# A conv-FFN up-projection with a second convolution buffer, an earlier copy-out and a reordered weight load

## The chip, the cores and the metric

The kernel runs on one core of a Trainium2 chip. The metric is the time of one execution on the device in microseconds, the median of several; lower is better. The core has five instruction queues: PE (matrix products, with its weight loads as PEld), DVE (vector), ACT (scalar), POOL (GpSimd) and SP, which here only issues DMAs. Each queue runs its instructions in order, and an instruction that has to wait for another engine holds up all that stands behind it in its own queue.

## The reference, cut to what matters

One layer of a hybrid streaming encoder, on 1024 prompt frames and 8 x 16 sampled frames (1152 rows in all, float32):

```python
mixed = sigmoid(gate_a) * o_gla + sigmoid(gate_b) * o_diff       # two token mixers
x = layer_norm(ALPHA * x + mixed @ w_out, ln1_g, ln1_b)          # (1152, 1024)

up = x @ w_up                                                    # (1152, 2 * 2816)
a, gate = split(up, [2816])
a_full = concat([left, a], axis=time)                            # two earlier rows
a_conv = conv_b
for j in range(3):
    a_conv = a_conv + a_full[:, j:j + t] * conv_w[j]
h = gelu(a_conv) * gate
x = layer_norm(ALPHA * x + h @ w_down, ln2_g, ln2_b)
```

The change lies in the middle part: from `x` after the first layer norm to `h`.

## The kernel before

Up to about 1,220 us the kernel computes the mixers; nothing of that is touched. Then come three stages.

**Output projection.** A loop over nine tiles `t` of 128 rows: `mixed @ w_out` on PE, `layer_norm`, transposes on PE, and copies of the transposed rows into the arrays from which the up-projection's moving operands are made. From `t = 4` on, four additions and subtractions per tile (L946 to L949, on POOL) combine the row halves in place (`rs1`, `r21`, `r11`, `r12`). Between the tiles the code already puts in pieces of the first two up-projection panels: `Panel(0)` (a weight load and two casts with their splits) at `t = 6`; `panels[0].sums()` (a second load and the weight sums) and `Panel(1)` at `t = 7`; the first and second product of panel 0 at `t = 8`, and the first product of panel 1 after it.

**Up-projection.** 22 panels `f` of 128 columns of `a` and 128 of `gate`. A panel is a two-by-two block scheme with seven products in place of eight. Every product has two halves `c`, four steps of depth, and three matmuls each (high and low parts of a float32 split): 24 matmuls of 128x288, so 168 in a panel. The sums over the product numbers are kept in PSUM: tile `ux` takes up products 1, 6, 7 and 4 in turn, `uy` product 2, `uz` products 5 and then 3. What is read out on the way:

- after product 1: `first_out` copies `ux` into the convolution's input `ab` on ACT (L798), and adds `uy` (product 2) on DVE (L800). Product 6 may not write over `ux` before the copy is done. Ahead of that the two left-edge columns are set on POOL (L795, L796).
- after product 6: ACT copies `ux` into the gate tile `gt` (L806); after product 7 again (L811), and DVE adds `uz` (L812).
- after product 4: ACT copies `ux` into the second half of `ab` (L815, L817); after product 3 DVE adds `uz` to `gt` (L819).
- then the convolution on DVE, `ab` to `cv` (L825 to L829), its gelu on ACT (L830), the product with `gt` on DVE (L831), and the store of `h_d[f]` (L832).

The weights of a panel are two loads of 512 KB, issued by SP (L746 and L758, three buffers in `wpool`), four sums on POOL (L762 to L765), and for each of the seven products a cast on ACT (L93) and a split on DVE (L96). The five weights of products 6, 5, 7, 4 and 3 go through a ring of `WV` buffers (tag `wv`), those of 1 and 2 through three (`w0`). There is one `ab` (pool `ue`), one `gt` and one `cv` (pool `uc`).

**Down-projection.** `h` is read back, cast and split (`hw`), and multiplied with `w_down` in six groups of panels, the first with two.

The order of each engine's queue is not the order of the code: the framework simulates the program on a timeline and sorts the instructions by it (`schedule_with_timeline_sim=True`); waits are put in afterwards. In the steady panels PE's queue before is, with the number of matmuls behind each product (n is a panel, n+1 the next): 5 of n, 24; 6 of n, 24; 2 of n+1, 11; 7 of n, 24; 2 of n+1, 11; 4 of n, 24; 3 of n, 24; 2 of n+1, 2; 1 of n+2, 24. In the code, `rest` runs from product 6 to the store.

## Time and profile before

| what | value |
|---|---|
| time, median of 3 runs (lowest to highest) | 2195.18 us (2193.39 to 2195.99) |
| the profiled execution | 2196.83 us |
| its span | 2195.1 us |
| granted clock of PE, mean | 0.984 |
| PE busy | 2083.5 us, 95% |
| PE weight loads busy | 1953.6 us, 89% |
| DVE busy | 1165.0 us, 53% |
| ACT busy | 785.0 us, 36% |
| POOL busy | 468.3 us, 21% |

The profiled execution lies 1.65 us above the median of the runs, and its span is 1.7 us shorter than its time. PE is busy for 95% of the span, so all that can be won without fewer matmuls is in the other 112 us and in stretches with a lower clock. The up-projection takes the span from about 1,337 to 1,899 us, the down-projection the rest. In the profile's rows a number such as `128x288` is a tile (partitions x elements); `[1.73 <-ACT ab L798]` says that the engine stood idle for 1.73 us just before, and that the event that ended it was the ACT instruction of line 798 that writes `ab`. Where a row ends in `x2`, two instructions are put together, and the duration is that of both.

### The profile page before, as it was taken

What the parts mean: (1) busy time and instruction counts of PE and PEld (TensorE: products, weight loads), DVE (VectorE), ACT (ScalarE), POOL (GpSimd) and SP (SyncE); (2) the same over time, 40 slices, a digit from 0 to 9 for tenths busy, and PEclk for the clock granted to TensorE, in tenths of its full rate; (3) what the DMA queues carried; (4) which work ended last, traced back from release to release, by engine and by line L of the source; (5) the groups of instructions that cost most, each with busy time, mean ns of one, the idle gap of its engine ahead of it and who ended that gap; (6) DMA issues with size and microseconds to landing.
All of it is one profiled execution on the core that took longest, in us unless ns stands there. A gap on an engine that the chain in (4) does not pass through costs nothing.

```text
span 2195.1 us, 34411 instructions
## 1 busy us (share of the span) xinstructions
PE 2083.5 (95%) x14088; PEld 1953.6 (89%) x14088; DVE 1165.0 (53%) x1848; ACT 785.0 (36%) x1750; POOL 468.3 (21%) x531
## 2 busy tenths in 40 slices
PE   7999999999999989999999895899999999999998
PEld 7999999899999989999999785899989999878886
DVE  4344443554536455554641666666666666554447
ACT  3233333344434444443644324333333333311122
POOL 0133242100120102101223025322332232000006
PEclk9999999999999999999999997999999999999999
DMA  5215322513052233314342531221212121452222
GB/s 173 55 24 113 96 75 78 134 30 97 25 133 59 59 71 71 94 46 85 58 79 100 185 115 58 62 78 60 71 60 81 61 70 61 164 172 82 82 72 87
DMA packets 187003, 185.31 MB, mean 84 GB/s; under 512 B 9318, under 2 KB 169428, under 8 KB 186830
## 3 DMA queue, kind: packets, MB, share of 16 engines
q1 hardware_dynamic: 186846, 183.11, 29.6%
q8 instruction: 111, 1.82, 0.3%
q14 instruction: 46, 0.38, 0.1%
HBM read 131.10 MB, written 51.98 MB: 83 GB/s over the span
## 4 chain that ended last, share of the span: by engine, by line
PE 50%; DVE 11%; DMA 5%; ACT 3%; issue 2%; POOL 1%; SPq 0%; DVEq 0%; ACTq 0%; POOLq 0%
PE mm L87 5%; PE mm L88 5%; PE mm L89 5%; PE ux L87 4%; PE dn L87 3%; PE dn L89 3%; PE dn L88 3%; PE ux L89 3%; PE ux L88 3%; DVE cv L828 3%; DVE wv L96 2%; PE po L657 2%; PE opp L87 1%; PE opp L89 1%; PE opp L88 1%
## 5 line engine op out<-in xcount | busy, mean ns | idle before, releaser
L88 PE MATMUL mm<-wlo,xh 128*128 128x256 f32 x1368 | 394.2, 288 | 0.6 <-DVE wlo L96 0.6
L89 PE MATMUL mm<-whi,xl 128*128 128x256 f32 x1368 | 394.1, 288 | 0.0
L87 PE MATMUL mm<-whi,xh 128*128 128x256 f32 x1368 | 393.4, 288 | 0.0
L87 PE MATMUL ux<-xh,wv 128*128 128x288 f32 x704 | 214.2, 304 | 54.8 <-ACT ab L798 32.7
L88 PEld LDWEIGHTS mm<-wlo,xh 128*128 128x128 f32 x1368 | 263.0, 192 | 3.1 <-issue 1.0
L89 PEld LDWEIGHTS mm<-whi,xl 128*128 128x128 f32 x1368 | 263.1, 192 | 2.3 <-issue 0.8
L87 PEld LDWEIGHTS mm<-whi,xh 128*128 128x128 f32 x1368 | 262.6, 192 | 2.5 <-issue 1.0
L88 PE MATMUL ux<-xl,wv 128*128 128x288 f32 x704 | 212.1, 301 | 0.0
L89 PE MATMUL ux<-xh,wv 128*128 128x288 f32 x704 | 211.6, 301 | 0.0
L87 PE MATMUL mm<-xh,whi 128*128 128x384 f32 x576 | 195.7, 340 | 3.5 <-ACT dq L233 3.3
L89 PE MATMUL mm<-xh,wlo 128*128 128x384 f32 x576 | 196.4, 342 | 0.0
L88 PE MATMUL mm<-xl,whi 128*128 128x384 f32 x576 | 196.4, 341 | 0.0
L87 PEld LDWEIGHTS ux<-xh,wv 128*128 128x128 f32 x704 | 136.1, 193 | 59.5 <-ACT ab L798 37.0
L87 PE MATMUL dn<-hw 128*128 128x512 f32 x396 | 154.2, 396 | 7.9 <-ACT hw L93 4.2
L88 PE MATMUL dn<-hw 128*128 128x512 f32 x396 | 155.3, 395 | 0.0
L89 PE MATMUL dn<-hw 128*128 128x512 f32 x396 | 153.3, 392 | 0.0
L88 PEld LDWEIGHTS ux<-xl,wv 128*128 128x128 f32 x704 | 136.4, 194 | 0.1
L89 PEld LDWEIGHTS ux<-xh,wv 128*128 128x128 f32 x704 | 136.3, 194 | 0.0
L632 ACT ACTIVATE e<-sc,mx 128x256 f32<-128x256 f32 (+7 forms) x128 | 94.0, 740 | 90.3 <-DVE mx L628 78.5
L701 POOL TENSOR_TENSOR gm<-gm,sg 128x512 f32<-128x512 f32 (+1 forms) x40 | 50.0, 1251 | 308.9 <-ACT sg L223 139.3
L87 PEld LDWEIGHTS mm<-xh,whi 128*128 128x128 f32 x576 | 108.6, 189 | 5.8 <-ACT dq L233 3.6
L96 DVE TENSOR_TENSOR wlo<-raw,whi 128x1024 fp32r<-128x1024 f32 x62 | 92.2, 1493 | 36.2 <-ACT whi L93 35.9
(325 smaller groups left out, 4778.6 us busy)
## 6 DMA issues: line engine op xcount, KB each, us to landing
fraw<-in_w_up SPq DMA_DIRECT2D x44, 512.0 KB, 3.9
raw<-in_w_in SPq DMA_DIRECT2D x38, 512.0 KB, 6.1
raw<-in_w_in SPq DMA_DIRECT2D x52, 256.0 KB, 6.1
h_d<-cv SPq DMA_DIRECT2D x22, 576.0 KB, 5.1
hr<-h_d SPq DMA_DIRECT2D x22, 576.0 KB, 3.7
fraw<-in_w_down SPq DMA_DIRECT2D x22, 512.0 KB, 4.4
og_d<-orow SPq DMA_DIRECT2D x4, 1152.0 KB, 11.3
od_d<-od SPq DMA_DIRECT2D x8, 576.0 KB, 4.5
```

What stands on the lines that cost most here:

```text
L87: nc.tensor.matmul(ps, lhsT=lh, rhs=rh, start=start, stop=False, skip_group_check=more)
L88: nc.tensor.matmul(ps, lhsT=lh, rhs=rl, start=False, stop=False, skip_group_check=more)
L89: nc.tensor.matmul(ps, lhsT=ll, rhs=rh, start=False, stop=stop, skip_group_check=more)
L96: V.tensor_tensor(lo, src, hi.bitcast(F32), ALU.subtract)
L632: act(e[:, :nk], scs[m][:, :nk], AF.Exp, bias=mx[:, m:m + 1], accum_out=Z[:, i, m:m + 1])
L657: nc.tensor.matmul(po[:, 0, :], lhsT=wT[:, kt, :], rhs=v[:, kt, vc0:vc0 + P], start=kt == 0, stop=kt == i)
L701: G.tensor_tensor(gv, gv, e, ALU.mult)
L828: V.scalar_tensor_tensor(cv[:, :SEQ], ab[:, j:j + SEQ], cw[:, j, f:f + 1], cv[:, :SEQ], ALU.mult, ALU.add)
```

## The change

Five things are edited.

1. `ab` alternates between two pools: panels with an odd number take it from `uc`, the others from `ue`, so that there are two buffers.
2. `first_out` is split: the copies of `ux` stay in it, the two additions of `uy` are in a new `second_out`. The calls are now `first_out`, `second`, `second_out`: the first product is copied out ahead of the second product.
3. The ring `wv` of weight buffers has six tiles, not seven (`WV = 6`).
4. `Panel(0)` stands at `t = 5` and `Panel(1)` at `t = 6`; `panels[0].sums()` stays at `t = 7`.
5. At the last tile of the output projection the four combinations of rows run on DVE and not on POOL.

```diff
@@ -42,7 +42,7 @@
 WB = 256
 HT = NTOK // 2
 HN = HT // 2
-WV = 7
+WV = 6
 PREP_AT = 6
 
 
@@ -790,12 +790,15 @@
 
         def first_out(self):
             f = self.f
-            self.ab = ab = ue.tile([P, SEQ + 2 + NS * 18], F32, tag="ab", name="ab")
+            self.ab = ab = (uc if f % 2 else ue).tile([P, SEQ + 2 + NS * 18], F32, tag="ab", name="ab")
             self.abs_ = ab[:, SEQ + 2:].rearrange("p (s c) -> p s c", c=18)
             G.memset(ab[:, 0:2], 0.0)
             G.tensor_copy(self.abs_[:, :, 0:2], ccT[:, f])
             for c in range(2):
                 nc.scalar.copy(ab[:, 2 + c * HN:2 + (c + 1) * HN], self.X[c][:, :HN])
+
+        def second_out(self):
+            ab = self.ab
             for c in range(2):
                 V.tensor_tensor(ab[:, 2 + c * HN:2 + (c + 1) * HN], ab[:, 2 + c * HN:2 + (c + 1) * HN], self.Y[c][:, :HN], ALU.add)
 
@@ -918,15 +921,15 @@
                     nxt = o_prep(t + 1)
                     rn = r_load(t + 1)
             layer_norm(op, r, g1, b1)
-            if t == 6:
-                panels[0] = Panel(0)
+            if t in (5, 6):
+                panels[t - 5] = Panel(t - 5)
             if t == 7:
                 panels[0].sums()
-                panels[1] = Panel(1)
             if t == NT - 1:
                 panels[0].first()
+                panels[0].first_out()
                 panels[0].second()
-                panels[0].first_out()
+                panels[0].second_out()
             nc.sync.dma_start(x1_d[t * P:(t + 1) * P, :], r)
             for j in range(2):
                 tp = otp.tile([P, 512], F32, tag="otp", name="otp").rearrange("p (i c) -> p i c", i=4)
@@ -943,10 +946,11 @@
                     nc.scalar.copy(R[f"r2{j + 1}"][:, :, b - HT:hi - HT], tp[:, :, b - lo:])
             if hi > HT:
                 c = slice(max(lo, HT) - HT, hi - HT)
-                G.tensor_tensor(R["rs1"][:, :, c], R["r21"][:, :, c], R["r22"][:, :, c], ALU.add)
-                G.tensor_tensor(R["r21"][:, :, c], R["r11"][:, :, c], R["r21"][:, :, c], ALU.subtract)
-                G.tensor_tensor(R["r11"][:, :, c], R["rs1"][:, :, c], R["r11"][:, :, c], ALU.subtract)
-                G.tensor_tensor(R["r12"][:, :, c], R["r12"][:, :, c], R["r11"][:, :, c], ALU.subtract)
+                E = V if t == NT - 1 else G
+                E.tensor_tensor(R["rs1"][:, :, c], R["r21"][:, :, c], R["r22"][:, :, c], ALU.add)
+                E.tensor_tensor(R["r21"][:, :, c], R["r11"][:, :, c], R["r21"][:, :, c], ALU.subtract)
+                E.tensor_tensor(R["r11"][:, :, c], R["rs1"][:, :, c], R["r11"][:, :, c], ALU.subtract)
+                E.tensor_tensor(R["r12"][:, :, c], R["r12"][:, :, c], R["r11"][:, :, c], ALU.subtract)
             if t == NT - 1:
                 panels[1].first()
 
@@ -972,8 +976,9 @@
         if f > 1:
             p.first()
         if f > 0:
+            p.first_out()
             p.second()
-            p.first_out()
+            p.second_out()
         p.rest()
     us_.close()
     xv_s.close()
```

Lines behind `first_out` have numbers that are 3 higher in the changed kernel (the copy to `gt`, L806, is L809; the additions of `uy`, L800, are L803; the gelu is L833, the product with `gt` L834, the store L835), and those of the row combinations 4 higher. Since the queues are sorted by a simulated timeline, they move in more places than the diff names. From about `t = 5` of the output projection on the order differs; ahead of that, and behind the first group of the down-projection, it is the same. In the steady panels PE's queue is now: 6 of n, 24 matmuls; 5 of n, 24; 7 of n, 24; 1 of n+1, 11; 4 of n, 24; 3 of n, 24; 1 of n+1, 13; 2 of n+1, 24. Three more places follow; a name such as `ab_15777` is one allocation of a tile, and `[waits PE_49]` names the engine that an instruction waits for.

ACT and then DVE in a steady panel, before; `ux_15751` and `ux_15752` are the two halves of panel n+1, `cv_15710` is the convolution of panel n, `gt_15574` its gate, `uy_15777` a half of product 2 of n+1:

```order
L93 CAST wv_15972<-ta_15966 128x512 [waits Pool_49]
L93 CAST wv_15975<-ta_15966 128x512 [waits PE_49]
L93 CAST wv_16194<-fraw_16192 128x512 [waits DMAHW2_49,PE_49]
L93 CAST wv_16197<-fraw_16192 128x512 [waits PE_49,Activation_49]
L830 ACTIVATE cv_15710<-cv_15710 128x1152 [waits DMAHW3_49,DVE_49]
L798 COPY ab_15803<-ux_15751 128x288 [waits Pool_49]
L798 COPY ab_15803<-ux_15752 128x288
L93 CAST wv_15978<-tb_15967 128x512 [waits PE_49]
L806 COPY gt_15810<-ux_15751 128x288 [waits DVE_49,PE_49]
```

```order
L96 TENSOR_TENSOR wv_16194<-fraw_16192,wv_16194 128x512 [waits DMAHW2_49,Activation_49]
L96 TENSOR_TENSOR wv_16197<-fraw_16192,wv_16197 128x512 [waits Activation_49]
L831 TENSOR_TENSOR cv_15710<-cv_15710,gt_15574 128x1152 [waits Activation_49]
L800 TENSOR_TENSOR ab_15803<-ab_15803,uy_15777 128x288 [waits Activation_49]
L800 TENSOR_TENSOR ab_15803<-ab_15803,uy_15778 128x288 [waits Activation_49]
```

The same in the changed kernel, where `uy_15782` is the half of product 2 of n+1:

```order
L93 CAST wv_15972<-ta_15966 128x512 [waits PE_49,Activation_49,Pool_49]
L798 COPY ab_15777<-ux_15751 128x288 [waits PE_49]
L798 COPY ab_15777<-ux_15752 128x288 [waits PE_49]
L93 CAST wv_15961<-fraw_15956 128x512
L833 ACTIVATE cv_15710<-cv_15710 128x1152 [waits DMAHW2_49,DVE_49]
L93 CAST wv_16194<-fraw_16192 128x512 [waits DMAHW3_49,PE_49,Activation_49]
L809 COPY gt_15810<-ux_15751 128x288 [waits DVE_49,PE_49]
L809 COPY gt_15810<-ux_15752 128x288 [waits PE_49]
```

```order
L96 TENSOR_TENSOR wv_15961<-fraw_15956,wv_15961 128x512 [waits PE_49,Activation_49]
L803 TENSOR_TENSOR ab_15777<-ab_15777,uy_15782 128x288 [waits PE_49]
L803 TENSOR_TENSOR ab_15777<-ab_15777,uy_15783 128x288 [waits PE_49]
L834 TENSOR_TENSOR cv_15710<-cv_15710,gt_15574 128x1152 [waits Activation_49]
L96 TENSOR_TENSOR wv_16194<-fraw_16192,wv_16194 128x512 [waits DMAHW3_49,Activation_49]
```

On ACT the two copies to `ab` (L798) stood behind the gelu and waited for POOL; now they stand ahead of it and wait for PE, with one weight cast in front of them that waits for PE, ACT and POOL. On DVE the two additions of `uy` stood behind the product with `gt` (L831); now they stand ahead of it (L834) and wait for PE.

POOL and then SP in a steady panel, before; `ta` and `tb` are the weight sums of one panel, `fraw` its two loads:

```order
L762 TENSOR_TENSOR ta_15966<-fraw_15964,fraw_15956 128x512 [waits DMAHW7_49,DMAHW1_49]
L764 TENSOR_TENSOR tb_15967<-fraw_15964 128x512
L821 COPY tails_78<-ab_15331 128x2 [waits Activation_49]
L822 COPY tails_78<-ab_15331 128x16 [waits Activation_49]
L763 TENSOR_TENSOR ta_15966<-fraw_15964,ta_15966 128x512 [waits Pool_49]
L765 TENSOR_TENSOR tb_15967<-fraw_15956,ta_15966 128x512 [waits Pool_49]
L795 MEMSET ab_15567 128x2 [waits DVE_49]
L796 COPY ab_15567<-ccT_77 128x8x2
```

```order
L746 DMA fraw_15956<-in_w_up 128x8x128 [waits DMAHW4_49,DMAHW7_49,DVE_49,Pool_49]
L832 DMA h_d_62<-cv_15238 128x1152 [waits DVE_49]
L758 DMA fraw_15964<-in_w_up 128x8x128 [waits DMAHW3_49,DVE_49]
```

And in the changed kernel:

```order
L795 MEMSET ab_15777 128x2 [waits DVE_49,Pool_49]
L796 COPY ab_15777<-ccT_77 128x8x2
L762 TENSOR_TENSOR ta_15966<-fraw_15964,fraw_15956 128x512 [waits DMAHW1_49,DMAHW0_49]
L764 TENSOR_TENSOR tb_15967<-fraw_15964 128x512
L763 TENSOR_TENSOR ta_15966<-fraw_15964,ta_15966 128x512 [waits Pool_49]
L765 TENSOR_TENSOR tb_15967<-fraw_15956,ta_15966 128x512 [waits Pool_49]
L824 COPY tails_78<-ab_15541 128x2 [waits Activation_49]
L825 COPY tails_78<-ab_15541 128x16 [waits Activation_49]
```

```order
L746 DMA fraw_15956<-in_w_up 128x8x128 [waits DMAHW3_49,DVE_49]
L758 DMA fraw_15964<-in_w_up 128x8x128 [waits DMAHW1_49,DMAHW5_49,DVE_49,Pool_49]
L835 DMA h_d_62<-cv_15474 128x1152 [waits DVE_49]
```

The same `ab` columns, sums and tails are set, but the left-edge columns of a later panel now stand ahead of the sums, and the copies of the tails, which wait for ACT, behind them. On SP the first load of a panel (L746) now waits for DVE alone and the second (L758) for DVE and POOL; before it was the other way round.

POOL at the turn from the output projection into the panels, before; `rs1`, `r21`, `r11` and `r12` are the combinations of tile 6 (its last two) and of tile 7, `fraw_13465` and `fraw_13358` the loads of panel 0, `fraw_13866` and `fraw_13473` those of panel 1:

```order
L765 TENSOR_TENSOR tb_13468<-fraw_13358,ta_13467 128x512 [waits Pool_49]
L948 TENSOR_TENSOR r11_12635<-rs1_12634,r11_12635 128x4x128 [waits Pool_49]
L949 TENSOR_TENSOR r12_12631<-r12_12631,r11_12635 128x4x128 [waits Pool_49]
L762 TENSOR_TENSOR ta_13868<-fraw_13866,fraw_13473 128x512 [waits DMAHW5_49,DMAHW7_49,DVE_49,PE_49]
L764 TENSOR_TENSOR tb_13869<-fraw_13866 128x512 [waits PE_49]
L763 TENSOR_TENSOR ta_13868<-fraw_13866,ta_13868 128x512 [waits Pool_49]
L946 TENSOR_TENSOR rs1_12634<-r21_12632,r22_12633 128x4x128 [waits Activation_49]
L765 TENSOR_TENSOR tb_13869<-fraw_13473,ta_13868 128x512 [waits Pool_49]
L947 TENSOR_TENSOR r21_12632<-r11_12635,r21_12632 128x4x128 [waits Pool_49]
L948 TENSOR_TENSOR r11_12635<-rs1_12634,r11_12635 128x4x128 [waits Pool_49]
L949 TENSOR_TENSOR r12_12631<-r12_12631,r11_12635 128x4x128 [waits Pool_49]
```

And in the changed kernel, where `fraw_13473` and `fraw_13259` are the loads of panel 0, `fraw_13866` and `fraw_13366` those of panel 1:

```order
L952 TENSOR_TENSOR r11_12635<-rs1_12634,r11_12635 128x4x128 [waits Pool_49]
L762 TENSOR_TENSOR ta_13475<-fraw_13473,fraw_13259 128x512 [waits DMAHW2_49,DMAHW5_49,DVE_49,PE_49]
L764 TENSOR_TENSOR tb_13476<-fraw_13473 128x512 [waits PE_49]
L953 TENSOR_TENSOR r12_12631<-r12_12631,r11_12635 128x4x128 [waits Pool_49]
L763 TENSOR_TENSOR ta_13475<-fraw_13473,ta_13475 128x512 [waits Pool_49]
L765 TENSOR_TENSOR tb_13476<-fraw_13259,ta_13475 128x512 [waits Pool_49]
L950 TENSOR_TENSOR rs1_12634<-r21_12632,r22_12633 128x4x128 [waits Activation_49]
L762 TENSOR_TENSOR ta_13868<-fraw_13866,fraw_13366 128x512 [waits DMAHW0_49,DMAHW7_49,DVE_49,PE_49]
L764 TENSOR_TENSOR tb_13869<-fraw_13866 128x512 [waits PE_49]
L951 TENSOR_TENSOR r21_12632<-r11_12635,r21_12632 128x4x128 [waits Pool_49]
L763 TENSOR_TENSOR ta_13868<-fraw_13866,ta_13868 128x512 [waits Pool_49]
```

The sums of panel 0 (L762 to L765) have gone from between the first combinations of tile 6 to behind them, and those of panel 1 from ahead of the combinations of tile 7 to between them. The four combinations of tile 8, which stood behind all this on POOL, are no longer in its queue.

## Rows read from the trace of the kernel before

**Rows 1.** Waits of PE, whole span: us in total, times, longest us.
```profile
PE ux L87 <- ACT ab L798: 32.7, 18, 2.3
PE ux L87 <- ACT wv L93: 22.1, 1, 22.1
```

**Rows 2.** Stretches: us, busy (count) PE, PEld, DVE, ACT, POOL, clock, DMA share, GB/s.
```profile
1572.30:1598.10 25.80, 24.07 (x168) 23.84 (x168) 15.77 (x21) 8.05 (x18) 7.50 (x8) 0.93 0.20 65
1598.10:1622.54 24.44, 22.54 (x169) 22.30 (x169) 15.95 (x21) 8.06 (x18) 7.46 (x8) 1.00 0.21 68
1399.36:1844.35 444.99, 414.56 (x3024) 410.51 (x3024) 284.34 (x361) 145.06 (x307) 138.66 (x144) 0.98 0.21 67
1844.35:1899.00 54.65, 54.65 (x410) 54.33 (x411) 24.95 (x43) 15.50 (x36) 2.64 (x10) 1.00 0.29 103
```

**Rows 3.** Order of time, PE, one panel: start us, duration us, instruction [idle].
```profile
1598.10 0.40 PE L87 MATMUL ux<-xh,wv 128*128 128x288 f32 x1 [1.73 <-ACT ab L798]
1598.34 0.29 PE L88 MATMUL ux<-xl,wv 128*128 128x288 f32 x1
...
1620.34 0.29 PE L89 MATMUL uz<-xh,wv 128*128 128x288 f32 x1
```

**Rows 4.** Order of time, ACT, POOL, DVE: panel at 1598, then at 1844 and 1866.
```profile
1611.05 0.27 ACT L817 COPY ab<-ux 128x128 f32<-128x128 f32 x1
...
1621.03 1.16 ACT L830 ACTIVATE cv<-cv 128x1152 f32<-128x1152 f32 x1 [2.87 <-DVE cv L829]
1622.10 0.68 ACT L798 COPY ab<-ux 128x288 f32<-128x288 f32 x2
...
1612.12 1.35 POOL L762 TENSOR_TENSOR ta<-fraw 128x512 f32<-128x512 f32 x1 [14.89 <-DMA fraw<-in_w_up]
...
1613.94 2.32 DVE L828 SCALAR_TENSOR_TENSOR cv<-ab,cw,cv 128x1024 f32<-128x1024 f32 x1
...
1622.23 1.36 DVE L831 TENSOR_TENSOR cv<-cv,gt 128x1152 f32<-128x1152 f32 x1
1623.51 0.81 DVE L800 TENSOR_TENSOR ab<-ab,uy 128x288 f32<-128x288 f32 x2
...
1857.30 0.27 ACT L817 COPY ab<-ux 128x128 f32<-128x128 f32 x1
...
1864.65 1.36 DVE L831 TENSOR_TENSOR cv<-cv,gt 128x1152 f32<-128x1152 f32 x1 [1.23 <-ACT cv L830]
...
1900.62 1.28 DVE L828 SCALAR_TENSOR_TENSOR cv<-ab,cw,cv 128x1024 f32<-128x1024 f32 x1
```

**Rows 5.** Order of time before the panels: SP, POOL, ACT, PE.
```profile
1309.16 0.38 SPq L758 DMA_DIRECT2D fraw<-in_w_up  x1
...
1321.89 0.38 SPq L746 DMA_DIRECT2D fraw<-in_w_up  x1
...
1332.26 0.38 SPq L758 DMA_DIRECT2D fraw<-in_w_up  x1
1345.56 0.38 SPq L746 DMA_DIRECT2D fraw<-in_w_up  x1
...
1343.27 2.26 POOL L765 TENSOR_TENSOR tb<-fraw,ta 128x512 f32<-128x512 f32 x1
...
1350.28 1.14 ACT L93 CAST wv<-fraw 128x512 fp32r<-128x512 f32 x2 [10.59 <-DMA fraw<-in_w_up]
...
1356.44 2.21 ACT L93 CAST xh<-r 128x1152 fp32r<-128x1152 f32 x2 [4.05 <-POOL r L948]
...
1367.64 0.61 PE L87 MATMUL ux<-xh,wv 128*128 128x288 f32 x1 [22.10 <-ACT wv L93]
```

**Rows 6.** Start of the down-projection: order of time (SP, PE); one stretch.
```profile
1904.77 0.32 SPq L832 DMA_DIRECT2D h_d<-cv  x1
...
1905.39 0.80 PE L87 MATMUL dn<-hw 128*128 128x512 f32 x1 [4.21 <-ACT hw L93]
...
1910.00:1920.00 10.00, 10.00 (x47) 8.12 (x46) 7.53 (x10) 4.07 (x4) 0.00 (x0) 0.94 0.97 326
```

## Prediction

> **What bounds the kernel now.** I read the waits of PE first. Of the whole span, one cause returns panel after panel: PE stands before the first matmul of product 6 and waits for the ACT copy of `ux` into `ab`, 18 times, 32.7 us in all, never over 2.3 us. The only longer wait stands once, 22.1 us ahead of the panels [rows 1]. So the stretch to look at is the up-projection, and the question is what the 18 waits cost with all that comes with them.
>
> For that I take the stretch from one such restart, 1399.36, to another, 1844.35: 444.99 us for 3024 matmuls, which are 18 panels of 168 [rows 2]. What would they take without a stall? Inside a panel the starts from 1598.34 to 1620.34 are 166 steps apart: 22.00 / 166 = 0.1325 us for one [rows 3]. 3024 x 0.1325 = 400.7 us, so 44.3 us are lost, 2.46 a panel. That is more than the recorded idle time, for two reasons. A restart costs a little more than its idle time shows, and in some panels the granted clock is below full: 24.07 us of PE busy at 0.93 against 22.54 at 1.00 [rows 2], 1.5 us each. Six of the 18 panels are like the one from 1572.30, some 9 us of the 44. That this can be had is shown by the last two panels: from 1844.35 to 1899.00 there is no wait, 410 matmuls in 54.65 us, 0.133 each, at clock 1.00 [rows 2].
>
> Why the wait stands there is seen in the order of time [rows 4]. After product 4 the last piece of `ab` is copied (1611.05); the convolution runs on DVE; its end releases both the gelu (1621.03, after 2.87 idle) and, through POOL's left-edge columns, the single `ab`; the copy stands behind the gelu on ACT and starts at 1622.10. PE, whose next step was due at 1620.34 + 0.13 [rows 3], starts where the stretch ends, at 1622.54. DVE is busy for 284 of the 445 us and ACT for 145 [rows 2], so neither is full: it is a chain, not a full engine.
>
> **Up-projection: what goes.** With two buffers and the copies ahead of the gelu, `ab` waits for the end of product 1 alone. In the new order of PE, counted from the end of product 4 of panel n: product 3, 24 matmuls, is done at 24 x 0.1325 = 3.2 us, product 1 of the next panel (13 more) at 4.9, product 2 (24) at 8.1, and there product 6 begins. The copies are 0.68 us for both [rows 4], so they are done at about 5.6 if nothing holds them, 2.5 us ahead of need.
>
> What can hold them is the cast in front of them on ACT, which waits for PE, ACT and POOL. With six buffers it takes over the one that product 3 of panel n read last, free at 3.2; that is early enough, and six buffers cost nothing as long as this is the last of its waits. Its POOL part, the weight sums, I place by the order: the second load now takes its buffer from the previous panel's first load, released at the end of the previous convolution; before, POOL sat 14.89 us until that load landed, in the middle of the convolution [rows 4]. So the sums move into the time between two convolutions, ahead of need. Behind this cast stand the copies and the gelu, and behind those the next panel's gate copies: if it came late, all of them would.
>
> **Up-projection: what is late next.** PE now needs, for product 7, the copy of product 6 into the single `gt`, and `gt` is free only after DVE's product with it. From the end of product 4 to product 7 PE has 24 + 13 + 24 + 24 + 24 = 109 matmuls, 14.4 us. Against that stands the chain: last copy at 1611.05, product with `gt` over at 1622.23 + 1.36 = 1623.59, 12.5 us [rows 4]. The two additions of `uy` now stand ahead of it, 0.81 us [rows 4], and the gate copy behind it, some 0.34 (half the pair of copies of the same shape): 13.7, so 0.7 us to spare. That is with POOL beside the convolution. Without, in the panel at 1857.30, the chain was 1864.65 + 1.36 - 1857.30 = 8.7 us [rows 4], and then product 2 sets it: the additions wait for it until 8.1, then 0.81 + 1.36 + 0.34, 10.7 with the trailing start. I take the chain between 10.7 and 13.7, nearer the lower end, and no wait. For the first two or three panels the order leaves only 97 matmuls, 12.9 us; there I allow 0.3 us each, 1 us in all.
>
> The term: 44.3 in the 18 panels, and the wait that ends at 1399.36, up to 2.3 [rows 1], less 1 us: **46 us gained**. If the dips of the clock stay though the waits go, 9 us of it stay too, and 37 remain.
>
> **The turn into the panels.** PE stands for 22.10 us until 1367.64 [rows 5]. Before it, in this order: the sums of panel 1 on POOL (1343.27, 2.26 us), the load of panel 2 that takes their buffer (SP, 1345.56), its two casts on ACT (1350.28, after 10.59 of waiting for the load), and behind them in ACT's queue the casts of the operand of product 6 (1356.44, after 4.05 more for POOL's combinations). The earlier `Panel(0)` and `Panel(1)` bring two first loads forward, but three buffers are all there are, so the second load of panel 0 goes from the place at 1309.16 to that at 1321.89, and the second load of panel 1 has no earlier place than 1332.26. The load of panel 2 therefore still leaves near 1345. The combinations of the last tile on DVE take away some of the 4.05. I take 1.5 us gained, between 1 lost (the sums of panel 1 one step later on POOL) and 5 gained (4.05 gone, and a little of the load).
>
> **The start of the down-projection.** PE begins at 1905.39 after 4.21 of waiting for the first casts, and the last `h_d` store leaves at 1904.77 [rows 6]. In the new order three of those casts stand ahead of the last gelu, so PE begins up to 4.2 us earlier; but the gelu and that store come 1 to 2 later, and from 1910 on DMA is busy at 0.97 with 326 GB/s [rows 6], so an early start can run into a later load. I take 3, between 0 and 4.2.
>
> **Sum.** 46 + 1.5 + 3 = 50.5. The profiled execution took 2196.83, so 2146.3 for one like it; it lay 1.65 above the median of the runs, so 2144.7, and I say **2145**.
>
> **Rivals.** *A, the forecast:* the waits go, 2136 to 2154, the upper end being the dips that stay. *B, the wait moves to the gate:* DVE still runs beside POOL, the 0.7 us to spare are not there, and half of the gain is given back in front of product 7: 2145 + 23 = 2168, from 2155 to 2178. For it speaks that L828 takes 2.32 us beside POOL and 1.28 in the last panel [rows 4]; against it that the sums move out of the convolution. *C, slower:* the same loop, longer than what it replaces. The panel lost 2.46 us; the loop would have to take 14.4 + 2.5 + 0.2 (the 4.5 us gained elsewhere over 20 panels) = 17.1 us before the whole became slower. At 17.5, three more vector operations lengthened by 1.04 each beside POOL on top of 13.7, and a gate cast behind them, PE waits 3.1 a panel: 20 x (3.1 - 2.46) - 4.5 = +8, 2203. No row shows a chain over 12.6 plus the two short terms, so it is unlikely. *D, the change does not do what it says:* the cast in front of the `ab` copies waits for a late load or late sums, and holds them until 2.5 us or more past their time, as the gelu did: then the 46 are gone and 2191 remain. *E, the shared port at the turn:* four combinations with two SBUF operands run on DVE beside POOL's sums of panel 1. The trace shows what such a meeting costs: 2.32 against 1.28 for L828 [rows 4], 1.04 more. Four times that is 4.2 us in the chain to product 6, so 2149.
>
> The Trainium skill speaks for E: SBUF — State Buffer, section Who interferes with whom, says that VectorE and GpSimd share one pair of ports, that a VectorE instruction with two SBUF inputs contends with a GpSimd one that reads SBUF, and that the other then fully blocks. The trace agrees in that L828 nearly doubled, by 1.04 us; whether the four combinations meet POOL no row of before can show.
>
> **Chances.** A 0.77, B 0.10, E 0.04, D 0.05, C 0.04. A and E and the lower part of B lie within 2134 to 2162, which leaves out D, C and half of B; the lower end is 5 gained at the turn, 4.2 at the end and the whole 46.6 without new waits. 0.2%, 4.4 us, is about what a measurement of this kernel can tell from no change. Faster 0.91 (A, B, E), same 0.05 (D), slower 0.04 (C).
>
> **What would show it.** Right: in the waits of PE the row for `ab` is gone or below 3 us; 18 steady panels take 401 to 406 us; in the order of time the copies to `ab` stand ahead of the gelu and start some 5 us after product 4; POOL's sums lie between the convolutions, and L831, as L828 is numbered there, takes 1.3 us in most panels; the turn is still near 20 us. Wrong: a row for `gt` in the waits of PE of 10 us or more (B, C), a row for `ab` or for `wv` of that size (D), or a clock near 0.93 in a panel without a wait, which would say that the dips did not come from the waits.

## The result and the profile after

| | before | changed |
|---|---|---|
| time, median | 2194.53 us (2193.39 to 2195.99, 4 runs) | 2145.68 us (2145.09 to 2148.87, 4 runs) |
| ratio | | 0.978, 95% interval 0.9763 to 0.9797 |
| the profiled execution | 2196.83 us | 2148.87 us |
| its span, granted clock | 2195.1 us, 0.984 | 2146.9 us, 0.988 |

The forecast was 2145. Where the 48.2 us between the two spans lie can be read off a few PE rows of both traces: the first store of the output projection as a mark, the last row of matmuls before the long gap (eight transposes), the first matmul after it, the last of the up-projection and the first of the down-projection.

| stretch of PE, us | before | changed | difference |
|---|---|---|---|
| start to the first store of the output projection | 1237.26 | 1241.20 | +3.94 |
| from there to the gap ahead of the panels | 107.24 | 107.42 | +0.18 |
| the gap (start of that last row to the next start) | 23.14 | 21.15 | -1.99 |
| the panels, to the last matmul of product 3 | 531.20 | 483.37 | -47.83 |
| from there to the first of the down-projection | 6.55 | 2.54 | -4.01 |
| the rest | 289.71 | 291.22 | +1.51 |

The first line holds instructions that the change does not touch. In the twelve further profiles below it lies between 1237.86 and 1240.56, so it is scatter of a single execution. Behind it the two profiles differ by 52.1 us; the medians of the runs differ by 48.9.

The waits of PE in the changed kernel (us in total, times, longest): the row for `ab` that led the list [rows 1] is gone.

```profile
PE ux L87 <- ACT wv L93: 20.1, 1, 20.1
...
PE ft L1024 <- DVE gt L822: 1.6, 1, 1.6
...
PE ux L87 <- ACT gt L809: 1.0, 1, 1.0
```

Stretches of the changed kernel, with the columns of [rows 2] (us; busy of PE, PEld, DVE, ACT, POOL; clock, DMA share, GB/s): all panels, then most of them, then the gap.

```profile
1369.77:1853.30 483.53, 482.58 (x3624) 482.12 (x3624) 293.01 (x430) 178.15 (x367) 147.70 (x164) 1.00 0.24 77
1446.33:1853.30 406.97, 406.97 (x3070) 406.74 (x3068) 238.36 (x359) 148.01 (x306) 117.85 (x136) 1.00 0.24 78
1349.59:1369.77 20.18, 0.13 (x3) 0.00 (x1) 15.13 (x14) 13.09 (x15) 5.93 (x6) 0.58 0.14 48
```

3070 matmuls in 406.97 us are 0.1326 each: PE's own pace, at clock 1.00. No steady panel shows the 0.93 any more.

One steady panel of the changed kernel in order of time (start, duration, idle before and its releaser), ACT, then DVE, then POOL. These rows answer to [rows 4].

```profile
1606.79 0.27 ACT L820 COPY ab<-ux 128x128 f32<-128x128 f32 x1
...
1610.39 0.39 ACT L798 COPY ab<-ux 128x288 f32<-128x288 f32 x1
...
1611.52 0.40 ACT L798 COPY ab<-ux 128x288 f32<-128x288 f32 x1 [0.74 <-PE ux L89]
...
1612.89 1.17 ACT L833 ACTIVATE cv<-cv 128x1152 f32<-128x1152 f32 x1 [0.45 <-DVE cv L832]
...
1616.52 0.40 ACT L809 COPY gt<-ux 128x288 f32<-128x288 f32 x1 [1.15 <-DVE cv L834]
...
1608.52 1.28 DVE L831 SCALAR_TENSOR_TENSOR cv<-ab,cw,cv 128x1024 f32<-128x1024 f32 x1
...
1614.70 0.45 DVE L803 TENSOR_TENSOR ab<-ab,uy 128x288 f32<-128x288 f32 x1 [0.89 <-PE uy L89]
...
1615.08 1.35 DVE L834 TENSOR_TENSOR cv<-cv,gt 128x1152 f32<-128x1152 f32 x1
...
1595.12 1.30 POOL L762 TENSOR_TENSOR ta<-fraw 128x512 f32<-128x512 f32 x1 [3.88 <-DMA fraw<-in_w_up]
...
1599.45 1.29 POOL L765 TENSOR_TENSOR tb<-fraw,ta 128x512 f32<-128x512 f32 x1
1606.96 0.19 POOL L824 COPY tails<-ab 128x2 f32<-128x2 f32 x1 [6.22 <-ACT ab L818]
```

Three things differ from before. The copies to `ab` stand ahead of the gelu. The weight sums on POOL (1595.12 to 1600.74) are over 6 us before the convolution begins. And so the convolution is short: L831 takes 1.28 us where L828 took 2.32 [rows 4], and the gelu starts 6.1 us after the last copy, not 10.0. Which of the three was needed was the question for the chip.

### The profile page after: what moved, and what is told of

Its sections match the earlier page's. It is cut to its first block, busy times and chain, and to the rows that moved or that the text cites. A ratio compares the mean times of both kernels' runs of the same rounds, so it can differ in the third digit from the quotient of the medians.

```text
span 2146.9 us, 34445 instructions
## 1 busy us (share of the span) xinstructions
PE 2070.8 (96%) x14088; PEld 1943.9 (91%) x14088; DVE 1130.8 (53%) x1852; ACT 789.7 (37%) x1750; POOL 456.0 (21%) x527
## 4 chain that ended last, share of the span: by engine, by line
PE 59%; DMA 5%; DVE 4%; issue 1%; ACT 1%; POOL 1%; SPq 0%; DVEq 0%; ACTq 0%; POOLq 0%
PE mm L88 5%; PE mm L87 5%; PE mm L89 5%; PE ux L87 4%; PE ux L89 4%; PE ux L88 4%; PE dn L89 3%; PE dn L87 3%; PE dn L88 3%; PE uz L88 2%; PE uz L87 2%; PE uz L89 2%; PE po L657 2%; PE opp L88 2%; PE opp L89 2%; PE opp L87 1%
## 5 line engine op out<-in xcount | busy, mean ns | idle before, releaser
L87 PE MATMUL ux<-xh,wv 128*128 128x288 f32 x704 | 207.2, 295 | 21.0 <-ACT wv L93 20.1
L89 PE MATMUL ux<-xh,wv 128*128 128x288 f32 x704 | 207.2, 295 | 0.0
L88 PE MATMUL ux<-xl,wv 128*128 128x288 f32 x704 | 207.1, 295 | 0.0
L87 PEld LDWEIGHTS ux<-xh,wv 128*128 128x128 f32 x704 | 132.3, 188 | 21.6 <-ACT wv L93 20.3
L89 PEld LDWEIGHTS ux<-xh,wv 128*128 128x128 f32 x704 | 132.0, 188 | 0.0
```

The lines of the kernel that those rows point to most:

```text
L87: nc.tensor.matmul(ps, lhsT=lh, rhs=rh, start=start, stop=False, skip_group_check=more)
L88: nc.tensor.matmul(ps, lhsT=lh, rhs=rl, start=False, stop=False, skip_group_check=more)
L89: nc.tensor.matmul(ps, lhsT=ll, rhs=rh, start=False, stop=stop, skip_group_check=more)
```

## Experiments

**Which edit removes the waits: the buffer, or the order of the calls.** Two kernels, each with one of them. The first is the kernel before with:

```diff
-WV = 7
+WV = 6
-            self.ab = ab = ue.tile([P, SEQ + 2 + NS * 18], F32, tag="ab", name="ab")
+            self.ab = ab = (uc if f % 2 else ue).tile([P, SEQ + 2 + NS * 18], F32, tag="ab", name="ab")
```

> The kernel before with only two things changed: ab alternates between two pools, and the weight ring has six buffers (with seven the second ab does not fit). The calls stay first, second, first_out; the first panels and the last combinations stay as before. Theory (the single buffer is the cause): the row of PE waiting for ab is gone, the up-projection takes 483 to 486 us as in the changed kernel, the turn about 22 us, in all 2146 to 2151. Rival (copying the first product out ahead of the second is the cause): the copies still stand behind the second product, most of the 18 waits stay, 2180 to 2194.

Measured: 2147.90 us (2144.52 to 2149.08), 0.9778 of the kernel before (0.9763 to 0.9792). No wait for `ab`; panels 482.44 us, gap 23.27. So far the theory holds. The second is the changed kernel with one buffer:

```diff
-            self.ab = ab = (uc if f % 2 else ue).tile([P, SEQ + 2 + NS * 18], F32, tag="ab", name="ab")
+            self.ab = ab = ue.tile([P, SEQ + 2 + NS * 18], F32, tag="ab", name="ab")
```

> The changed kernel with one thing taken back: ab comes from one pool again, so there is one buffer. Copies ahead of the second product, six weight buffers, early first panels and the last combinations on DVE stay. Theory (the single buffer is the cause): 18 waits for ab of about 33 us come back, the up-projection takes about 531 us; only the turn and the tail can gain, 2188 to 2195. Rival (the order of the calls is the cause): 2146 to 2152.

Measured: 2148.43 us (2144.85 to 2151.87), 0.9777 (0.9759 to 0.9795). The waits did not come back; panels 484.71. Here the theory fell: the buffer is not needed. Nor is it the order of the calls, since the first kernel did without that. In the second kernel the copies stand behind the gelu, as before, and PE does not wait for them. What the two have in common is six weight buffers, and sums that do not meet the convolution.

**The six weight buffers alone.** The kernel before with `WV = 6` and nothing else.

> The kernel before with one number changed: six weight buffers, not seven. One ab, the old order of the calls, the old first panels. Theory now (the waits come from POOL's weight sums running beside the convolution on DVE; with six buffers the split of product 3's weight comes later, and with it the second load and the sums, so that they fall behind the convolution): the 18 waits are gone, 2147 to 2152. Rival (the run before gained by its order of calls, copies ahead of the second product): 2188 to 2196.

Measured: 2149.50 us (2146.64 to 2151.36), 0.9777 (0.9763 to 0.9792); panels 484.54, one wait of 0.3 for `ab`. The panels' whole gain comes from one number. The trace shows how. Order of time in this kernel, ACT and POOL:

```profile
1612.13 0.27 ACT L817 COPY ab<-ux 128x128 f32<-128x128 f32 x1
1612.29 0.64 ACT L93 CAST wv<-fraw 128x512 fp32r<-128x512 f32 x1
...
1619.14 1.16 ACT L830 ACTIVATE cv<-cv 128x1152 f32<-128x1152 f32 x1
1620.22 0.68 ACT L798 COPY ab<-ux 128x288 f32<-128x288 f32 x2
...
1618.16 1.84 POOL L762 TENSOR_TENSOR ta<-fraw 128x512 f32<-128x512 f32 x1 [4.97 <-DMA fraw<-in_w_up]
```

And in the kernel before, ACT and SP, ahead of the last copy at 1611.05 [rows 4]:

```profile
1606.51 0.62 ACT L93 CAST wv<-fraw 128x512 fp32r<-128x512 f32 x1
...
1607.88 0.37 SPq L758 DMA_DIRECT2D fraw<-in_w_up  x1
```

The `wv<-fraw` cast is that of product 3's weight, the last reader but one of a load buffer (its split on DVE follows). With seven buffers it ran 4.5 us before the last copy to `ab`, and the next load left at 1607.88, landed, and started POOL's sums at 1612.12, 1.1 us after that copy: in the convolution. With six the cast stands behind the copies, the load leaves at 1614.02, and the sums start 6.0 us after the last copy, when the convolution is nearly over. The gelu then starts after 7.0 us, the `ab` copies end at 1620.90, and PE needs them 74 matmuls, 9.8 us, after product 4: at 1621.55. POOL's sums now meet the product with `gt` (L831 takes 2.45 us where it took 1.36 [rows 4]), which PE does not wait for.

**The sums, moved by hand.** If the meeting of POOL and DVE is the cause, moving the sums alone must do it, with seven buffers. A rule for the issue order in `sums()` of the kernel before, by which the four sums are queued on POOL behind the `memset` of the panel two before (`marks` keeps that instruction):

```diff
+            after = marks.get(("memset", self.f - 2))
+            with tc.issue_after(after.ins) if after is not None else ExitStack():
-            G.tensor_tensor(ta[:, 0, :], b12, b11, ALU.subtract)
+                G.tensor_tensor(ta[:, 0, :], b12, b11, ALU.subtract)
...
-            G.memset(ab[:, 0:2], 0.0)
+            marks["memset", f] = G.memset(ab[:, 0:2], 0.0)
```

> The kernel before, seven weight buffers and one ab, with one rule for the order of POOL: the four weight sums of a panel are queued behind the setting of the left-edge columns of the panel two before it, which waits for the end of a convolution, so they run between two convolutions. Theory (sums beside the convolution are the cause): the 18 waits are gone, 2146 to 2152. Rival (the number of weight buffers is the cause in itself, by the casts on ACT): the waits stay, 2188 to 2196.

Measured: 2148.24 us (2146.73 to 2149.74), 0.9773 (0.9753 to 0.9792); panels 483.73. The theory holds. And the opposite, the sums queued behind the first copy of the tails (`marks["tails", f]`), so that they run beside the convolution: with one buffer and `WV = 6`,

> The kernel before with six weight buffers and one ab, and the sums queued behind the first copy of the tails, so beside the convolution. Theory (sums beside the convolution, with one buffer, are the cause): the waits for ab are back although there are six weight buffers, 2185 to 2205. Rival (six weight buffers gain by themselves): 2147 to 2152.

Measured: 2179.96 us (2179.72 to 2180.21), 0.9917 (0.9897 to 0.9937); panels 512.20. Waits of PE in this kernel (us in total, times, longest):

```profile
PE ux L87 <- ACT ab L802: 19.1, 20, 1.9
...
PE uz L87 <- DVE gt L823: 2.1, 9, 0.3
```

The direction is the theory's, the size was over-estimated: each wait is some 0.8 to 1.0 us, not 1.8, since here the gelu starts 9.1 us after the last copy and not 9.8, and no panel loses clock. So with six buffers the meeting costs the panels 512.20 - 484.54 = 27.7 us, with seven 531.20 - 483.73 = 47.5. And with two buffers:

> The changed kernel, two ab buffers, with the opposite rule: the four weight sums of a panel are queued on POOL behind the first copy of the tails of the panel two before it, which waits for the last copy to ab, so they run beside the convolution. Theory (two buffers take the convolution out of PE's way, and the gate loop at 13.7 us fits into 14.4): no waits, 2146 to 2152. Rival (with the sums there the casts and the gate come late whatever the buffers): waits for ab or gt come back, 2165 to 2200.

Measured: 2147.05 us (2145.66 to 2148.99), 0.9765 (0.9749 to 0.9781); panels 484.56, no wait for `ab`. POOL and then ACT in this kernel:

```profile
1606.62 1.79 POOL L766 TENSOR_TENSOR ta<-fraw 128x512 f32<-128x512 f32 x1
...
1612.63 1.29 POOL L769 TENSOR_TENSOR tb<-fraw,ta 128x512 f32<-128x512 f32 x1
...
1606.32 0.27 ACT L824 COPY ab<-ux 128x128 f32<-128x128 f32 x1
...
1609.49 0.40 ACT L802 COPY ab<-ux 128x288 f32<-128x288 f32 x1 [2.39 <-PE ux L89]
1612.59 0.62 ACT L93 CAST wv<-ta 128x512 fp32r<-128x512 f32 x1 [2.69 <-POOL ta L767]
1613.11 0.40 ACT L802 COPY ab<-ux 128x288 f32<-128x288 f32 x1
```

The sums run right through the convolution, and the cast that waits for them does hold the second `ab` copy, until 1613.51; product 6 starts near 1614.1, so there was 0.6 us to spare. The four cells:

| panels, us | sums beside the convolution | sums outside it |
|---|---|---|
| one `ab` | 531.20 (before, seven weight buffers), 512.20 (six) | 484.54 (six), 483.73 (seven) |
| two `ab` | 484.56 | 483.37 (the changed kernel) |

Either cure is enough for the panels, and the second adds nothing there. But the second buffer does not come alone. In the steady panels of every kernel here with two buffers, except those with longer ACT work at the end of this section, the sorted queues also put the copies ahead of the gelu, and PE's product 6 comes 61 matmuls (8.1 us) after product 4, not 74 (9.8 us) as in all kernels with one. So the lower row is the buffer together with those orders; no run has it with both of the old ones. The length of the large convolution step says the same (one line each, least, mean and most in ns; before, then seven buffers with the sums moved out):

```profile
L828 DVE SCALAR_TENSOR_TENSOR cv<-ab,cw,cv x32: 1271/2012/2323, 1441.9 to 1815.5; 128x1024 f32<-128x1024 f32 x32
...
L832 DVE SCALAR_TENSOR_TENSOR cv<-ab,cw,cv x34: 1273/1277/1281, 1455.9 to 1814.1; 128x1024 f32<-128x1024 f32 x34
```

The second number is a median over both steps of a panel: 2.01 against 1.28. The Trainium skill (SBUF — State Buffer, Who interferes with whom) says that a VectorE instruction with two SBUF inputs contends with a GpSimd one that reads SBUF; the trace agrees: beside POOL's sums the step takes some 0.7 to 1.0 us longer.

**The turn.** Each of the two edits there taken back by itself: `Panel(0)` and `Panel(1)` at tiles 6 and 7 again, and the last combinations on POOL again (`E = G`).

> The changed kernel with Panel(0) and Panel(1) back at tiles 6 and 7. Theory (the turn hangs on the load of panel 2, which needs the buffer that the sums of panel 1 free): no more than 2 us either way, 2144 to 2148, PE idle at the turn 19 to 23 us. Rival (the earlier loads are what shortened the turn): PE idle at the turn 22 us or more and the time 2148 to 2151.

Measured: 2145.97 us (2143.45 to 2147.55), 0.9770 (0.9756 to 0.9785), gap 21.40.

> The changed kernel with the last tile's four combinations back on POOL. Theory (on DVE the third combination stands behind the split of panel 2's first weight and so waits for that load anyway): the turn within 1 us of the changed kernel's 20 us, 2145 to 2147. Rival (DVE is what shortens the turn): the casts of product 6's operand start 3 to 4 us later, PE idle about 23 us, 2148 to 2150. Rival (the shared port: on DVE they cost more than on POOL): 1 to 4 us faster than the changed kernel, 2142 to 2145.

Measured: 2144.55 us (2144.12 to 2148.55), 0.9769 (0.9754 to 0.9784), gap 19.89. By the times the two cannot be told from the changed kernel. By the gap, in one profile each:

| gap, us | combinations on POOL | on DVE |
|---|---|---|
| panels at 6 and 7 | 23.14 (before), 23.27, 23.26, 23.12 and 22.85 (four of the above) | 21.40 |
| panels at 5 and 6 | 19.89 | 21.15 (changed), 21.09 and 21.17 (two of the above) |

Both edits shorten it, by 3.3 and 1.7, and together they give less than the first alone. The changed kernel's rows say why (DVE, then ACT, then SP), and last come ACT and POOL of the kernel with the combinations on POOL:

```profile
1351.51 1.63 DVE L951 TENSOR_TENSOR r<-r,r 128x512 f32<-128x512 f32 x1
1357.18 0.69 DVE L96 TENSOR_TENSOR wv<-fraw,wv 128x512 fp32r<-128x512 f32 x1 [4.05 <-ACT wv L93]
1357.79 0.68 DVE L952 TENSOR_TENSOR r<-rs,r 128x512 f32<-128x512 f32 x1
...
1356.54 1.14 ACT L93 CAST wv<-fraw 128x512 fp32r<-128x512 f32 x2 [6.15 <-DMA fraw<-in_w_up]
1358.57 2.21 ACT L93 CAST xh<-r 128x1152 fp32r<-128x1152 f32 x2 [0.89 <-DVE r L952]
...
1352.62 0.38 SPq L746 DMA_DIRECT2D fraw<-in_w_up  x1
...
1355.32 2.21 ACT L93 CAST xh<-r 128x1152 fp32r<-128x1152 f32 x2
1354.02 1.27 POOL L952 TENSOR_TENSOR r<-rs,r 128x512 f32<-128x512 f32 x1
```

On DVE the third combination (L952) stands behind the split of panel 2's weight, which waits for its cast, which waits for the load that left at 1352.62. On POOL only sums and other combinations stand in front of it, and the `xh` casts follow those of panel 2 without a wait, where the changed kernel has 0.89. POOL does lengthen the combinations on DVE: L951 takes 1.63 us, the same step 0.69 in the kernel with the panels at 6 and 7, where POOL is done by then. But DVE then stands idle for 4.05 us all the same, so the loss is the queue's and not the port's.

**A version from this.** Two edits are made at the turn on top of the changed kernel: panel 2's casts are queued behind the operands' casts, and the weights of products 6 and 5 of panel 0 go into free buffers of another pool, so that their casts need not wait for memory which the row halves still hold. `xlast` is the last of the operands' casts; a weight that is already made is not made again (not shown).

```diff
             if t == 7:
                 panels[0].sums()
+                for (i, src), tag in zip(panels[0].T[:2], ("whi", "wlo")):
+                    panels[0].weight(wpool, tag, 3, i, src)
...
-            for i, src in ((1, ra[:, :512]), (2, ra[:, 512:])):
-                self.weight(ue, "w0", 3, i, src)
+            with tc.issue_after(xlast.ins) if f == 2 else ExitStack():
+                for i, src in ((1, ra[:, :512]), (2, ra[:, 512:])):
+                    self.weight(ue, "w0", 3, i, src)
```

> The changed kernel once more, as a base for the next runs on the same chip: 0.978 of the kernel before, some 2146 to 2150.

> The changed kernel with two edits at the turn: the weights of products 6 and 5 of panel 0 are put into the free third buffers of the weight sums (so that their casts need not wait for the memory of the row halves), and the two weight casts of panel 2 are queued on ACT behind the ten casts of the products' operands (so that neither ACT nor, through the split, DVE's combinations wait for panel 2's load). Theory (the turn is these two queues, not the combinations and not the port): PE idle at the turn falls from 21 to some 8 to 12 us in pieces, the time 8 to 12 us under the changed kernel of the same call. Rival (what the casts wait for is only renamed, as the ten casts of 11 us stand in PE's way in any case): within 3 us of the changed kernel.

Measured: the changed kernel 2147.02 us (2144.19 to 2150.68), 0.9782 (0.9768 to 0.9795); with the two edits 2140.30 us (2136.28 to 2142.45), 0.9744 (0.9730 to 0.9758). It beats both kernels, by 6.7 us the changed one, less than the 8 to 12 expected. Where PE begins, in this kernel:

```profile
1354.87 0.85 PE L87 MATMUL ux<-xh,wv 128*128 128x288 f32 x2 [6.89 <-ACT xh L93]
1356.26 0.61 PE L88 MATMUL ux<-xl,wv 128*128 128x288 f32 x1 [0.54 <-DVE xl L96]
```

The gap fell from 21.02 us in its base to 7.93, 13.1 less, but the panels took 489.85 against 481.89: the first products now run at the pace of the operands' casts and wait twice more (1.5 for a split, 2.7 for the gate). The rest after the first matmul of the down-projection took 294.30 against 290.02. There PE waits 8.2 us for DVE against 5.6, and the granted clock of the first 40 us is 0.87 against 0.91; what brings that about, no run shows.

**How much room the gate has.** Copies of `cv` onto itself behind the gelu lengthen the way to the product with `gt`: three, then six.

```diff
             act(cv, cv, AF.Gelu_apprx_tanh)
+            for _ in range(3):
+                nc.scalar.copy(cv, cv)
```

> The changed kernel with three more ACT copies of the whole cv onto itself behind the gelu, some 1.1 us each by the gelu of the same size; the result is the same. Theory (the gate loop ends 4 us ahead of product 7): the 3.5 us and a weight cast or two among them fit in, no waits, within 3 us of the changed kernel. Rival (the gate was about to be the next limit, 0.7 us to spare as the prediction's upper chain has it): 3 us a panel, some 55 us more.

Measured: 2196.52 us (2192.13 to 2201.44), 1.0006 (0.9994 to 1.0018). The expectation failed, and in the steady panels not by the gate. With the longer ACT work the simulated timeline sorted ACT's queue as before: gelu first, copies to `ab` behind it. ACT, the restart of PE, a step of DVE, and two rows of PE's waits in this kernel:

```profile
1615.70 1.17 ACT L833 ACTIVATE cv<-cv 128x1152 f32<-128x1152 f32 x1 [2.02 <-DVE cv L832]
1616.77 0.68 ACT L798 COPY ab<-ux 128x288 f32<-128x288 f32 x2
1617.34 2.35 ACT L835 COPY cv<-cv 128x1152 f32<-128x1152 f32 x2
...
1617.20 0.40 PE L87 MATMUL ux<-xh,wv 128*128 128x288 f32 x1 [1.00 <-ACT ab L798]
...
1609.73 1.45 DVE L829 TENSOR_SCALAR cv<-ab,cw,cb 128x128 f32<-128x128 f32 x1
...
PE dn L87 <- DVE yacc L1047: 14.6, 2, 12.2
PE ux L87 <- ACT gt L809: 10.9, 3, 9.8
```

There are two buffers, and the wait for `ab` is back, 17 times, 20.1 us. A second buffer does nothing for a copy that stands behind the gelu in its queue. Two more things are in this wait: product 6 comes 61 matmuls after product 4, 1.7 us sooner than in the old order, and POOL's last sums meet the first steps of the convolution (L829 takes 1.45 us here and 0.34 in the changed kernel). Besides, PE waits 9.8 us for the gate once, in the last panel, where no other product is left to fill in, and 12.2 us in the down-projection for `yacc` on DVE. How much of the gate's room three copies would use in the changed kernel's order is left open by this run.

> The same with six more copies, in place of three. By the queue of ACT they bring some 9 us with the casts and copies that stand among them, so the loop from the last copy to ab to the gate copy is some 18.5 us against 14.4: PE waits 4 us a panel for gt, 2215 to 2240, slower than the kernel before. Rival (the order gives way, or PE's other products fill in): under 2190.

Measured: 2291.55 us (2291.21 to 2291.89), 1.0435 (1.0416 to 1.0454). The mechanism as expected, the price not. ACT's end of the loop, PE's restart, then a whole panel and its first part, each as a stretch:

```profile
1591.80 0.28 ACT L820 COPY ab<-ux 128x128 f32<-128x128 f32 x1
...
1609.99 0.70 ACT L809 COPY gt<-ux 128x288 f32<-128x288 f32 x2 [1.42 <-DVE cv L836]
...
1610.45 0.61 PE L87 MATMUL ux<-xh,wv 128*128 128x288 f32 x1 [4.41 <-ACT gt L809]
...
1610.45:1639.63 29.18, 25.15 (x169) 24.92 (x169) 12.47 (x20) 14.59 (x24) 5.94 (x8) 0.90 0.17 56
...
1610.45:1614.00 3.55, 3.55 (x15) 3.55 (x16) 0.00 (x0) 0.51 (x2) 1.73 (x2) 0.50 0.65 239
```

The loop from the last copy to PE's restart is 1610.45 - 1591.80 = 18.65 us against 14.4, and PE waits 3.6 to 4.4 a panel, 13.3 in the last, 90.1 in 20 waits. But this panel takes 29.18 us, 6.9 more than 22.3: after the wait the granted clock is 0.50, 1.2 GHz, for 3.5 us, so the 169 matmuls are busy for 25.15 us, 2.9 more than at 1.00. Six of the 18 steady panels are like it; the other twelve take 27.6 to 28.5 us, with a clock of 0.92 to 0.94 and PE busy 1.5 to 1.8 us more.

## Why the prediction came out right, and where its reasons did not

**The terms.** Panels: 46 forecast, 47.8 measured. Turn: 1.5 forecast, 2.0. Start of the down-projection: 3 forecast, 4.0 at its first matmul, with 1.5 more in the rest. In the other profiles the kernels with two buffers begin it after 2.54 us or less and those with one after 6.55, while the rest is 286.8 to 290.3 with one buffer and 290.0 to 291.9 with two (without the last three kernels): by the means, 2.3 us are given back. What PE waits for there in the kernels with two buffers is the copy to `tr` on DVE (4.6 us in two waits in the changed kernel, 0.3 or none in those with one); ahead of one of the two DVE itself stands for 1.95 us behind a store. That the busy DMA [rows 6] is the reason is not shown. The sum of 50.5 stands against 48.2 in the spans, with 3.9 lost in an untouched part, and 48.9 in the medians. The turn's size came out partly by luck: the load of panel 2 was to leave where it did, and it left 4.0 us after the gap began (1352.62), not 1.1 [rows 5]; what made up for it is that the wait ahead of the operands' casts fell from 4.05 to 0.89 us, and that ACT's last two copies to the row halves and part of the load's time left the chain.

**Sound steps.** The loss to be won, 44.3 us by the pace of the last two panels, is the loss that went. The dips of the clock went with the waits, so the 9 us belonged to the term and not to the range. In the changed kernel the chain is as told: copies 3.9 and 5.0 us after product 4, the loop to the end of the product with `gt` 1616.43 - 1606.79 = 9.6 us and to the end of the first gate copy 10.1, a little under the 10.7 of the lower end, and set by product 2 (the addition at 1614.70 waits for it). The sums lie between convolutions, as the order had said.

**The step that failed is the cause.** The prediction gave the 46 us to the two buffers and to the copies ahead of the gelu, and counted six buffers as no cost and no gain. On the chip six buffers alone gain all of it (2149.50), and two buffers add nothing to the panels that can be measured once the sums are out of the way. The text had both halves in hand: it saw that the sums would move out of the convolution, and that L828 takes 1.04 us more beside POOL, but used them only for the gate, as a second chain's slack. It did not put the shorter convolution into the first chain. There the arithmetic was to be had: gelu at 10 us less some 3, plus gelu and copies 1.84, is under the 9.8 us that PE leaves in the old order. It is over the 8.1 us of the changed kernel's order, so there the copies ahead of the gelu are what carries the panels, as the prediction has it; but that tighter order comes with the second buffer, and with one buffer the kernel gained as much as the runs can tell (2148.43). So the number was right because each of two sufficient cures was in the change, and it says nothing of which one the change needed.

**Rivals.** B (the wait moves to the gate) did not come: one wait of 1.0 us. D's mechanism, a cast that waits for the sums and holds the copies, is there in the kernel with the sums forced in, 2.69 us of ACT's time, and still 0.6 us short of PE. E's meeting is there (L951 takes 1.63 us), but it is hidden: DVE is the worse place by 1.2 us with the early panels, by its queue and not by the port. C's mechanism was made by hand in the last run and its price was too low: it counted the waits only, and the clock took another 1.5 to 2.9 us a panel.

**Open:** whether two buffers would do for the panels and the tail without the orders of ACT and PE that go with them, what the busy DMA takes back in the rest, and why the faster version loses 4.3 us there.

## What to carry to other kernels

When an engine waits on a chain, take the chain's longest members and ask what runs beside them: here 3 us of a 10 us convolution were POOL's, and any edit that moved POOL's work, even one that only took away a buffer, was worth as much as a second buffer for the data. With an order that a program sorts, a change of a buffer count is a change of the order; read the queues before crediting the edit, and test each edit by itself before calling one the cause. A fix by a buffer holds only as long as the instruction is not queued behind the one it was freed from.

## What the runs showed of the hardware that was not expected

- **Waits of about 1 us left the clock alone, waits of 4 us halved it.** With waits of 0.8 to 1.0 us in every panel but the first (the kernel with one buffer and the sums forced in) and of 0.9 to 1.7 (the one with three more copies) the granted clock of the steady panels stays at 1.00. With 1.7 to 2.3 us, before, six of 18 panels fell to 0.93 [rows 2], and the length of the wait does not tell them apart: 1.75 us ahead of the panel at 1572.30, which fell, and 1.73 ahead of the one at 1598.10, which did not. With 3.6 to 4.4 us all 18 steady panels show 0.90 to 0.94, and 0.50 to 0.60 in the 3.5 us after the wait.
- **Fewer buffers, faster.** Counted from the last copy to `ab`, seven weight buffers let a cast go 4.7 us and a load 5.1 us earlier than six; six alone were 2.2% faster.
- **A stretch that nothing touches scatters by 4 us** between single executions (1237.26 to 1241.20), as much as two of the effects sought here; terms of that size were read from gaps, not from times.
